# Reordering the projections around a hyena stage: memory products moved to the upper half's columns, backward states to the lower half's last columns, q taken last

## The chip, the cores and the metric

One core of a Trainium2 chip runs the whole layer. The engines are TensorE (PE, with its weight loads shown apart as PEld), VectorE (DVE), ScalarE (ACT), GpSimd (POOL) and SyncE (SP), whose queue issues most of the transfers; ScalarE's queue issues the others. The metric is the device time of one execution in microseconds; the time of a kernel is the median of its runs.

## The reference

A bidirectional encoder layer over 2048 tokens of width 1024, in float32. What matters here:

```python
u = _rms_norm(h, norm_mix_g[l])
proj = u @ w_in[l]                                    # hyena z, x1, x2 | q, k | v, o | gates
hy = _short_conv_centred(proj[..., :HY_COLS], ...)    # width 3, over tokens
y_hy = _group_rms_norm(_hyena(hy, spec, hy_skip[l]), hy_norm_g[l], HYENA_GROUPS)
qk = jax.nn.silu(_short_conv_centred(proj[..., HY_COLS:off], ...))
y_ml = _mlstm_bidirectional(q, k, v, o_pre, gates, ml_gate_b[l])   # chunkwise scan, both directions
h = h + concat(y_hy, y_ml) @ w_out[l]
h = h + _cross_attention(_rms_norm(h, norm_x_g[l]), _rms_norm(mem, norm_mem_g[l]), wq, wk, wv, wo)
h = h + jnp.square(jax.nn.relu(_rms_norm(h, norm_ff_g[l]) @ ff_w1[l])) @ ff_w2[l]
```

The hyena is two rounds of long convolution by Fourier transform, each multiplied by a gate (x1, then x2). The mLSTM is a linear recurrence over chunks of 128 tokens with a matrix state per head, once forward and once backward. The cross-attention reads 256 memory tokens; its key and value weights depend on the memory alone.

## The kernel before, in words

Every large product is split into a high and a low part in fp32r and done as three matmuls (`mm3`, L340 to L342). So each set of weights (`weights`, L359) is loaded in pieces of 256 KB, rounded to its high part on ScalarE and reduced to its low part on VectorE (`split`, L345). `stream` (L378) keeps one set ahead of the one in use, and the tags `wh` and `wl` have two buffers, so two sets exist at a time. The list `items` in `inproj_open` fixes the order in which sets are taken, and each consumer takes the next.

The work is written as Python generators, which yield a weight for what they have just emitted; `weave` (L1923) alternates between two of them by the ratio of the weights done, `among` (L1977) takes one step of a second generator after every few of the first. This gives the order of the program. A scheduler with a timing model then orders each engine's instructions: an instruction that comes later in the program can go first where the earlier one isn't ready. A few instructions are pinned to program order among themselves.

The input projection holds half of the tokens (1024) at a time as a split operand `xh`, `xl`. `sweep` (L657) computes groups of 256 columns with channels on partitions: for each group four blocks (two token halves by two column halves), each of 24 matmuls of 512 columns; then the short convolution (L704 to L711), and `sweep_out` (L714) for the store, put off by `pending` until a later block. Column groups 0 to 5 are the hyena inputs (4 and 5 are the gate x2), 6 and 7 are q, 8 and 9 are k. `natural` (L759) computes a group of 256 columns with tokens on partitions, eight row tiles of 24 matmuls with 256 columns: groups 0 and 1 are v, 2 and 3 are the output gate o, 3 with the gate columns. A natural group is called a natural tile below.

`memproj` (L602) works on the memory. For each of four heads and for keys, then values, a projection (`project`, 48 matmuls of 256 columns) is multiplied by a second set of weights (`keys`: 48 of 256 columns; `values`: 24 of 512) and stored as `gd` or `vw`, which attention reads as weights. The eight projections with their eight products take sixteen sets of weights of 1 MB.

`gates` prepares gate rows and columns for the mLSTM. `backward` (L1097) steps through the chunk states of the backward direction, from chunk 15 down, and stores each one: two transfers in, one product with the gate on GpSimd, eight matmul records (L1082), four VectorE updates (L1088), one transfer out. `mlstm` (L1115) then loads packed rows (L1142) and goes through chunks 0 to 15 with both directions at once: loads, scores (L1175), values and states (L1213, L1215), the forward state update, a norm.

Before, the order is: sweeps of groups 0 to 3 for both halves; then, woven with hyena by 279 to 499: groups 4 to 9 of the upper half, naturals 3, 0, 1, 2 of the upper half, natural 3 of the lower half, groups 4 to 9 of the lower half with a gate step after every third block, naturals 0 and 1 of the lower half, natural 2 and the first three projections with two key products, with the states of chunks 15 to 8 (`far_states`, L1111, pinned) among these. Behind hyena come the other memory products, woven with `mlstm`: first the states of chunks 7 to 1, whose old state is read back from memory (`old_state`), then chunks 0 to 4. The tiles of `mlstm` lie in the memory that hyena has used. Attention comes next, woven with the remaining chunks; it starts from the hyena half of its first 512 tokens and needs chunks 0 to 3 for the other half.

Of the kernel before, what the change touches and what calls it, by code (L numbers as in the profile page):

```python
# [10 lines left out]
F32 = mybir.dt.float32  # L11
# [9 lines left out]
D = 1024  # L21
# [112 lines left out]
class Prog:  # L134
# [249 lines left out]

    NAT_AT = {0: 2}

    def inproj_open(self, es):
# [195 lines left out]

    def prep_mem(self):
        sb = self.isb
        self.memt = [[sb.tile([128, 1088], F32R, tag=tag, name="mt", bufs=2)[:, 0:D].rearrange("p (k t) -> p k t", k=4)
                      for tag in ("P", "cv")] for h in range(2)]

        def load(h):
            t = sb.tile([128, D], F32, tag="xn", name="xt", bufs=2).rearrange("p (k t) -> p k t", k=4)  # L590
            self.nc.sync.dma_start(out=t, in_=self.a["mem_t"].rearrange("(k p) t -> p k t", p=128)[:, 4 * h:4 * h + 4])
            return t

        def halves():
            xs = [load(h) for h in range(2)]
            rb = self.spread(self.diagonal(self.rm))
            for h in range(2):
                self.scaled(xs[h], 4 * h, self.g_mem, rb, *self.memt[h])
                yield
        self.prepq = halves()  # L600

    def memproj(self):  # L602
        nc, sb = self.nc, self.isb
        gd = self.dram("gd", (2, 128, 8, 512))
        vw = self.dram("vw", (4, 128, 8, 256))
        self.pop(2)
        mt = self.memt

        def project():
# [6 lines left out]
            t = sb.tile([128, 2, 2, 256], F32R, tag="xn", name="kt", bufs=2)  # L616
            self.split(t[:, 0], t[:, 1], p)
            return t
# [471 lines left out]

    def old_state(self, sb, n):
        t = sb.tile([128, 4, 129], F32, tag="cf", name="cb", bufs=3)
        cbd = self.dram("cbd", (15, 128, 516))
        self.nc.sync.dma_start(out=t.rearrange("d h e -> d (h e)"), in_=cbd[n - 1])
        return t

    def backward(self, sb, first, last, old, pin=None, lean=False):  # L1097
# [12 lines left out]

    def far_states(self):  # L1111
        with self.tc.tile_pool(name="m_b", bufs=1, side="right") as sb:
            yield from self.backward(sb, 15, 7, None, self.tc.keep_in_program_order, True)

    def mlstm(self, es):  # L1115
# [23 lines left out]
        for s in range(2):  # L1139
# [801 lines left out]
def program(p):  # L1941
    with ExitStack() as ms:
        with ExitStack() as es:
            p.inproj_open(es)
            p.filters_open()
            p.prepq = p.x_first()
            p.pop()
            s = chain(p.sweep(range(4), 0, True, lambda: p.prep_x(1)), p.sweep(range(4), 1, False))
            next(s)
            next(s)  # L1950
            weave(s, p.filters(), 140, 80, True)
            p.gates_open(ms)
# [70 lines left out]
```

## Time and profile before

| What | Value |
|---|---|
| median of 3 runs | 3175.22 us (3166.64 to 3175.26) |
| the profiled execution | 3178.03 us |
| its span, first to last instruction | 3176.3 us |
| PE busy | 3039.3 us, 96% |
| PEld busy | 2393.8 us, 75% |
| DVE busy | 2048.0 us, 64% |
| ACT busy | 1503.0 us, 47% |
| POOL busy | 1157.8 us, 36% |
| mean granted clock of TensorE | 0.982 |
| moved by the DMA engines | 609.48 MB, 192 GB/s |

The page cuts the span into 40 slices of 79.4 us and gives for each the busy tenths of an engine, the granted clock and the DMA share. A second view gives busy times for any stretches; others list instructions in order of time, group them by line and shape, or tell for a tile what its instructions waited for. A wait is put down to the instruction that released it. Busy times of matmuls overlap, since their ends are modelled, so a price for TensorE is best taken from one start to the next.

### The profile page before, as it was taken

The page shows a single profiled execution, that of the slowest core. Times are in us where ns is not written, and L with a number is a line of the kernel's source. Part 1 is how long each engine was busy: PE and PEld are TensorE (multiplying, and loading weights), DVE is VectorE, ACT ScalarE, POOL GpSimd, SP SyncE. Part 2 cuts the span into 40 slices and gives each one's busy share as a digit, 9 for nine tenths or more (in the row PEclk, how much of TensorE's full clock was granted, in tenths as well). Part 3 has the DMA queues.
Part 4 walks back from the last instruction along what each step waited for, and adds up shares of the span by engine and source line. Part 5 has one row for each costly group of instructions (what it writes and reads, how often), then busy time and mean ns, then how long its engine had stood idle before and what let it go on. Part 6 is the DMA issues. An engine that isn't in the chain of part 4 may idle for free.

```text
span 3176.3 us, 43590 instructions
## 1 busy us (share of the span) xinstructions
PE 3039.3 (96%) x14473; PEld 2393.8 (75%) x14473; DVE 2048.0 (64%) x3563; ACT 1503.0 (47%) x2873; POOL 1157.8 (36%) x802
## 2 busy tenths in 40 slices
PE   6999999999999976999999999999999999999998
PEld 4655566776668766788888888888888878888876
DVE  7775466434865676878766566657655686565695
ACT  5543366523675343445454455556555443333335
POOL 0122012100112334324231426776555483434483
PEclk9999999999999998999999999999999999999999
DMA  5554767686576988547374747656644474444434
GB/s 190 191 196 162 255 194 205 180 253 212 165 226 191 309 256 263 172 144 231 114 272 144 274 131 246 203 194 221 216 155 146 163 243 147 144 129 152 123 93 169
DMA packets 447673, 609.48 MB, mean 192 GB/s; under 512 B 39118, under 2 KB 249166, under 8 KB 446424
## 3 DMA queue, kind: packets, MB, share of 16 engines
q1 hardware_dynamic: 409268, 548.18, 54.7%
q10 hardware_dynamic: 38180, 58.51, 5.5%
q8 instruction: 115, 1.88, 0.2%
q14 instruction: 110, 0.90, 0.1%
HBM read 404.15 MB, written 202.41 MB: 191 GB/s over the span
## 4 chain that ended last, share of the span: by engine, by line
PE 79%; DMA 8%; DVE 7%; issue 3%; ACT 2%; POOL 1%; SPq 0%; ACTq 0%; DVEq 0%; POOLq 0%
PE mm L340 17%; PE mm L342 17%; PE mm L341 17%; PE hy L342 5%; PE hy L340 5%; PE hy L341 5%; PE hy L177 3%; PE hy L876 2%; PE mm L845 2%; PE hy L918 1%; DMA xt<-in_x_t_dram 1%; DVE wl L345 1%; PE hy L1213 1%; PE hy L1082 1%; PE hy L1215 1%
## 5 line engine op out<-in xcount | busy, mean ns | idle before, releaser
L345 DVE TENSOR_TENSOR wl<-wn,wh 128x512 fp32r<-128x512 f32 (+1 forms) x364 | 289.5, 830 | 128.9 <-ACT wh L345 128.7
L1558 DVE TENSOR_TENSOR bl<-wr,bh 128x512 fp32r<-128x512 f32 x213 | 239.1, 1129 | 130.8 <-ACT bh L1557 130.6
L1557 ACT CAST ah<-w 128x512 fp32r<-128x512 f32 x284 | 176.7, 623 | 303.3 <-PE hy L341 156.1
L345 ACT CAST wh<-wn 128x512 fp32r<-128x512 f32 (+1 forms) x364 | 208.1, 619 | 218.7 <-PE mm L342 51.2
L923 POOL TENSOR_TENSOR b<-b,a 128x512 f32<-128x512 f32 x64 | 87.2, 1363 | 586.8 <-ACT b L921 463.2
L340 PE MATMUL mm<-xh,wh 128*128 128x512 f32 x640 | 271.6, 425 | 3.7 <-ACT xh L500 2.3
L341 PE MATMUL mm<-xl,wh 128*128 128x512 f32 x640 | 257.9, 404 | 2.4 <-DVE xl L345 1.8
L342 PE MATMUL mm<-xh,wl 128*128 128x512 f32 x640 | 259.2, 405 | 0.0
L1557 ACT CAST bh<-wr 128x512 fp32r<-128x512 f32 x232 | 143.7, 621 | 233.3 <-PE mm L342 181.1
L1558 DVE TENSOR_TENSOR al<-w,ah 128x512 fp32r<-128x512 f32 x236 | 214.4, 909 | 54.3 <-ACT ah L1557 52.9
L342 PE MATMUL mm<-bh,al 128*128 128x512 f32 x576 | 225.3, 394 | 7.3 <-DVE al L1558 4.7
L340 PE MATMUL mm<-bh,ah 128*128 128x512 f32 x576 | 226.9, 394 | 1.0 <-DVE acc L1715 0.9
L341 PE MATMUL mm<-bl,ah 128*128 128x512 f32 x576 | 226.1, 393 | 0.0
L340 PE MATMUL mm<-act,wh 128*128 128x512 f32 x512 | 198.4, 393 | 2.6 <-ACT wh L345 1.3
L341 PE MATMUL mm<-act,wh 128*128 128x512 f32 x512 | 200.4, 392 | 0.2 <-DVE act L345 0.2
L342 PE MATMUL mm<-act,wl 128*128 128x512 f32 x512 | 199.0, 391 | 0.0
L340 PE MATMUL hy<-bh,ah 128*128 128x512 f32 x448 | 175.2, 391 | 0.0
L341 PE MATMUL hy<-bl,ah 128*128 128x512 f32 x448 | 174.6, 390 | 0.0
L342 PE MATMUL hy<-bh,al 128*128 128x512 f32 x448 | 174.4, 390 | 0.0
L340 PEld LDWEIGHTS mm<-xh,wh 128*128 128x128 f32 x640 | 122.0, 191 | 65.7 <-issue 29.2
L341 PEld LDWEIGHTS mm<-xl,wh 128*128 128x128 f32 x640 | 121.6, 190 | 53.0 <-issue 24.4
L323 POOL TENSOR_TENSOR b<-b 128x512 f32<-128x512 f32 x32 | 59.1, 1848 | 275.8 <-DVE P L685 127.8
(378 smaller groups left out, 8487.2 us busy)
## 6 DMA issues: line engine op xcount, KB each, us to landing
wr<-hc SPq DMA_DIRECT2D x224, 256.0 KB
w<-in_ff_w_dram SPq DMA_DIRECT2D x172, 256.0 KB
hc<-wn SPq DMA_DIRECT2D x128, 256.0 KB
wn<-in_w_in_dram SPq DMA_DIRECT2D x100, 256.0 KB
hc<-q SPq DMA_DIRECT2D x96, 256.0 KB
fs<-a SPq DMA_DIRECT2D x32, 512.0 KB
a<-fs SPq DMA_DIRECT2D x64, 256.0 KB
a<-zs SPq DMA_DIRECT2D x64, 256.0 KB
```

The costliest lines, as they stand in the source:

```text
L177: b = self.nc.tensor.matmul(*products[-1], start=True, stop=True)
L323: nc.gpsimd.tensor_tensor(e[1], f, b, ALU.subtract)
L340: mm(ps, lh, rh, start=start, stop=False)
L341: mm(ps, lh, rl, start=False, stop=False)
L342: mm(ps, ll, rh, start=False, stop=stop)
L345: both = (self.nc.scalar.copy(hi, src), self.nc.vector.tensor_tensor(lo, src, hi.bitcast(F32), ALU.subtract))
L845: nc.tensor.matmul(pp, dm[:, m], t[:, m], start=True, stop=True)
L876: nc.tensor.matmul(pg, em[:, m], y, start=True, stop=True)
L918: nc.tensor.matmul(pp, dm[:, m], t[:, m], start=True, stop=True)
L923: nc.gpsimd.tensor_tensor(xt, xt, hi[:, m], ALU.mult)
L1557: self.nc.scalar.copy(hi, src)
L1558: eng.tensor_tensor(lo, src, hi.bitcast(F32), ALU.subtract)
```

## The change

- The memory's scaled operand (`mem_operand`, before `prep_mem`) gets tiles of its own in a pool beside hyena's, in place of the convolution's tags.
- All eight projections, the four key products and the value products of heads 0 and 1 are taken between the blocks of groups 4 to 9 of the upper half, one step after every third block (`both`). The projections of heads 2 and 3 for the values are stored (`vt`), and read back, split and multiplied behind hyena.
- The lower half's groups go 4, 5, 8, 9 (x2, k), with a gate step after every second block; then naturals 0 and 1 (v), with seven steps of backward states between; then groups 6 and 7 (q), with one step after each block. All fifteen states run there, pinned, without reading an old state back.
- Behind hyena stay natural 2 of the lower half and the two value products, beside chunks 0 to 4. The last store of q is flushed ahead of `mlstm`, which no longer steps through states.
- The ratios of `weave` follow: 279 to 565, and 38 to 48 behind hyena.

```diff
-        mem = first[:1]
-        for i in range(8):
-            mem += ([nat[self.NAT_AT[i]]] if i in self.NAT_AT else []) + first[i + 1:i + 2] + second[i:i + 1]
-        items = tr[:4] * 2 + tr[4:] + [nat[c] for c in (3, 0, 1, 2, 3)] + tr[4:] + nat[:2] + mem
+        (c4, c5, c6, c7, c8, c9), f, w = tr[4:], first, second
+        items = tr[:4] * 2 + [c4, c5, f[0], c6, f[1], w[0], f[2], w[1], c7, f[3], w[2], c8, f[4], w[3]]
+        items += [c9, f[5], w[4], f[6], w[5], f[7]] + [nat[c] for c in (3, 0, 1, 2, 3)]
+        items += [c4, c5, c8, c9] + nat[:2] + [c6, c7, nat[2]] + w[6:]
...
-    def prep_mem(self):
+    def mem_operand(self, pool):
         sb = self.isb
-        self.memt = [[sb.tile([128, 1088], F32R, tag=tag, name="mt", bufs=2)[:, 0:D].rearrange("p (k t) -> p k t", k=4)
-                      for tag in ("P", "cv")] for h in range(2)]
+        self.memt = [[pool.tile([128, 4, 256], F32R, name=f"mt{x}{h}") for x in "hl"] for h in range(2)]
...
+            if keep is not None:
+                nc.scalar.dma_start(out=vt[keep], in_=staged(p).rearrange("p i t -> p (i t)"))
+                return None
...
-        t = project()
-        for i in range(8):
-            if i in self.NAT_AT:
-                yield from self.natural(0, (self.NAT_AT[i],))
-            yield 11
-            nxt = project() if i < 7 else None
-            (keys if i < 4 else values)(i % 4, t)
-            t = nxt
+        with self.tc.tile_pool(name="m_t", bufs=1, side="right") as pool:
+            self.mem_operand(pool)
+            yield 0
+            t = project()
+            for i in range(6):
+                yield 11
+                nxt = project() if i < 5 else project(0)
+                (keys if i < 4 else values)(i % 4, t)
+                t = nxt
+            project(1)
+        yield 6
+        for i in range(2):
+            st = sb.tile([128, 512], F32, tag="st", name="st", bufs=3)
+            nc.sync.dma_start(out=st, in_=vt[i])
+            t = pair()
+            self.split(t[:, 0], t[:, 1], st.rearrange("p (i t) -> p i t", i=2))
+            values(2 + i, t)
+            yield 8
...
-    def far_states(self):
+    def back_states(self):
         with self.tc.tile_pool(name="m_b", bufs=1, side="right") as sb:
-            yield from self.backward(sb, 15, 7, None, self.tc.keep_in_program_order, True)
+            yield from self.backward(sb, 15, 0, None, self.tc.keep_in_program_order, True)
...
-        for _ in self.backward(sb, 7, 0, self.old_state(sb, 8)):
-            yield 3
...
-            n = p.memproj()
+            n, states = p.memproj(), p.back_states()
             with ExitStack() as hs:
                 weave(p.hyena(hs),
-                      chain(s, p.sweep(range(4, 10), 1, True), p.natural(1, (3, 0, 1, 2), lambda: p.prep_x(0)),
-                            p.natural(0, (3,)), among(p.sweep(range(4, 10), 0, False), p.gates(), 3),
-                            among(chain(p.natural(0, (0, 1), p.prep_mem, 2), take(n, 5)), p.far_states(), 1)),
-                      279, 499)
+                      chain(s, both(p.sweep(range(4, 10), 1, True), 3, take(n, 8)), p.natural(1, (3, 0, 1, 2), lambda: p.prep_x(0)),
+                            p.natural(0, (3,)), among(p.sweep((4, 5, 8, 9), 0, False), p.gates(), 2),
+                            both(p.natural(0, (0, 1)), 1, take(states, 7), 2), both(p.sweep((6, 7), 0, False), 1, states)),
+                      279, 565)
+            p.flush()
             m = p.mlstm(ms)
-            weave(n, take(m, 13), 85, 75)
-            for _ in take(m, 1):
-                pass
+            weave(chain(p.natural(0, (2,)), n), chain((12,), take(m, 6)), 38, 48)
...
+def both(g, n, h, m=1):
+
+    for i, v in enumerate(g):
+        yield v
+        if i % n == n - 1:
+            yield from take(h, m)
+    yield from h
```

More of the change, by code (lines that the diff above doesn't have):

```diff
@@ L383, in stream @@
         yield cur
-    NAT_AT = {0: 2}
     def inproj_open(self, es):
@@ L592, in load @@
             return t
[L594 to L600, printed above, removed]
+        xs = [load(h) for h in range(2)]
+        rb = self.spread(self.diagonal(self.rm))
+        for h in range(2):
+            self.scaled(xs[h], 4 * h, self.g_mem, rb, *self.memt[h])
     def memproj(self):
@@ L605, in memproj, with pair, project @@
         vw = self.dram("vw", (4, 128, 8, 256))
-        self.pop(2)
-        mt = self.memt
-        def project():
+        vt = self.dram("vt", (2, 128, 512))
+        def pair():
+            return sb.tile([128, 2, 2, 256], F32R, tag="xn", name="kt", bufs=2)
+        def project(keep=None):
+            mt = self.memt
             wh, wl = next(self.wst)
@@ L615, in project @@
                     self.mm3(p[:, m], wh[:, k, ms], wl[:, k, ms], mt[k // 4][0][:, k % 4], mt[k // 4][1][:, k % 4], k == 0, k == 7)
-            t = sb.tile([128, 2, 2, 256], F32R, tag="xn", name="kt", bufs=2)
+            if keep is not None:
+                nc.scalar.dma_start(out=vt[keep], in_=staged(p).rearrange("p i t -> p (i t)"))
+                return None
+            t = pair()
             self.split(t[:, 0], t[:, 1], p)
@@ L646, in values @@
                     nc.scalar.dma_start(out=vw[2 * d:2 * d + 2, :, 2 * h + mt].rearrange("i p c -> p i c"), in_=o)
-        t = project()
-        for i in range(8):
-            if i in self.NAT_AT:
-                yield from self.natural(0, (self.NAT_AT[i],))
-            yield 11
-            nxt = project() if i < 7 else None
-            (keys if i < 4 else values)(i % 4, t)
-            t = nxt
+        with self.tc.tile_pool(name="m_t", bufs=1, side="right") as pool:
[12 more added lines that the diff above has]
+            nc.sync.dma_start(out=st, in_=vt[i])
+            t = pair()
+            self.split(t[:, 0], t[:, 1], st.rearrange("p (i t) -> p i t", i=2))
+            values(2 + i, t)
+            yield 8
     def sweep(self, cols, hf, first, after=None):
@@ L1089, in update @@
                                                pc[:, 129 * i:129 * i + 129], ALU.mult, ALU.add)
[L1091 to L1095, printed above, removed]
     def backward(self, sb, first, last, old, pin=None, lean=False):
```

## The prediction

> **What bounds the kernel now.** I read the slices of the page first, then the busy table by stretches, then the instructions of TensorE and of SyncE's queue in order of time, and last the waits by tile. The slices show where TensorE is not full (slices of 79.4 us; busy tenths, then the granted clock):
>
> ```profile
> PE   6999999999999976999999999999999999999998
> ...
> PEclk9999999999999998999999999999999999999999
> ```
>
> Apart from the start there is one hole, in the fifteenth and sixteenth slice, 1112 to 1270 us. The same place by stretches, with one earlier stretch beside it for comparison (columns: length, then busy us and instructions of PE, weight loads, DVE, ACT, POOL; clock, DMA share, GB/s):
>
> ```profile
> core 0: us, PE busy (x) PEld busy (x) DVE busy (x) ACT busy (x) POOL busy (x), PEclk, DMA share, GB/s
> 1029.00:1157.00 128.00, 114.34 (x791) 96.24 (x790) 95.00 (x209) 45.14 (x85) 44.49 (x28) 0.96 0.93 283
> 1157.00:1230.00 73.00, 57.64 (x325) 50.31 (x323) 42.14 (x117) 32.03 (x80) 26.60 (x25) 0.88 0.93 292
> 1230.00:1285.00 55.00, 33.09 (x184) 30.46 (x184) 39.61 (x137) 19.47 (x82) 23.10 (x19) 0.69 0.62 199
> 340.00:510.00 170.00, 161.25 (x617) 105.73 (x610) 94.92 (x141) 96.09 (x154) 19.00 (x14) 0.98 0.75 232
> ```
>
> From 1029 to 1157 the memory products run beside the end of hyena, with the DMA engines at 0.93: TensorE is idle 13.7 us. From 1157 to 1285 it is idle 15.4 + 21.9 = 37.3 us, and its clock falls to 0.88 and 0.69. That second part is a chain, seen in the DMA queue of SyncE (start, us taken to issue):
>
> ```profile
> 1155.24 1.09 SPq L955 DMA_DIRECT2D yh<-a  x2
> ...
> 1160.06 7.44 SPq L1142 DMA_DIRECT2D rows<-rows  x8
> ...
> 1169.18 0.43 SPq L1064 DMA_DIRECT2D kn<-kn  x1
> ...
> 1203.91 0.33 SPq L1107 DMA_DIRECT2D cbd<-cb  x1
> 1204.28 0.43 SPq L1149 DMA_DIRECT2D qn<-qt  x1
> ```
>
> Hyena stores its last rows at 1155. Then come the packed rows (1160), then seven backward states one after the other (first load 1169, last store 1204), and only then the loads of chunk 0. TensorE's own order says what follows:
>
> ```profile
> 1223.44 0.39 PE L1213 MATMUL hy<-va,rw 128*128 128x129 f32 x2
> ...
> 1232.81 0.39 PE L1213 MATMUL hy<-va,rw 128*128 128x129 f32 x2
> ...
> 1254.15 0.64 PE L1213 MATMUL hy<-va,rw 128*128 128x129 f32 x2
> ...
> 1264.28 0.77 PE L1213 MATMUL hy<-va,rw 128*128 128x129 f32 x2 [1.23 <-issue]
> ...
> 1279.33 2.44 PE L1350 MATMUL hy<-ident,wn 128*128 128x128 f32 x16
> ...
> 1285.19 0.73 PE L340 MATMUL mm<-act,wh 128*128 128x512 f32 x2 [1.22 <-ACT act L345]
> ```
>
> Chunks 1 to 4 begin at 1223, 1233, 1254 and 1264, 9 to 21 us apart, and the first product of attention at 1285. So 1204 to 1285, 81 us, is five chunks by their own latency; the memory products that could cover it have run out by 1230.
>
> **The change, part by part.** Prices of TensorE work at full clock are spacings from start to start:
>
> ```profile
> 1002.05 0.28 PE L340 MATMUL mm<-wh,xh 128*128 128x256 f32 x1
> 1002.17 0.28 PE L341 MATMUL mm<-wl,xh 128*128 128x256 f32 x1
> ```
>
> and from the chain that ended last (start, us):
>
> ```profile
> 1151.21 0.21 PE mm L340
> ...
> 1005.59 0.89 PE hy L1082 x8
> ```
>
> 0.12 us for 256 columns, 0.215 for 512, 0.9 for one state. A projection or a key product is 48 x 0.12 = 5.8 us, a value product 24 x 0.215 = 5.2, a natural tile 192 x 0.12 = 23, a chunk about 5.3 (scores and state 0.9 each, 32 records at 0.11 between 1223.44 and the end of its group).
>
> 1. *What lies behind hyena's end.* Before, between 1157 and 1285:
>
> ```profile
> L1082 PE MATMUL hy<-ve,kn 128*128 128x129 f32 x96 | 17.1, 337 | 16.3 <-issue 9.7 <-POOL ve L1078 6.4 <-ACT hy L1218 0.2
> ...
> L342 PE MATMUL mm<-mt,wl 128*128 128x256 f32 x32 | 10.9, 342 | 0.6 <-DVE wl L345 0.2
> ...
> L340 PE MATMUL mm<-wh,kt 128*128 128x512 f32 x27 | 9.9, 449 | 0.8 <-ACT wh L345 0.8
> ```
>
> That is two projections (32 records of each of three kinds), most of four value products, seven states and five chunks: 11.6 + 20.8 + 6.3 + 26.5 = 65 us of work in 128. After, one natural tile, two value products and five chunks: 23 + 10.4 + 26.5 = 60. So only 5 us net moves ahead of hyena's end (+5); the gain cannot come from less work there but from a shorter chain.
>
> 2. *Seven states leave that chain.* They go beside the columns, so the 35 us from 1169 to 1204 fall away (-35). The 12 us from 1157 to 1169 (rows, masks) and the 81 us from loads to attention stay: 93 in place of 128. The reload of a stored state goes too; it is one DMA and inside the 35.
>
> 3. *q is now last, and chunk 0 reads it back.* The price of that trip (ns, min/median/max):
>
> ```profile
> L707 DVE SCALAR_TENSOR_TENSOR cv<-P,par,cv x9: 1286/1290/2359, 802.2 to 960.1; 128x1040 f32<-128x1040 f32 x9
> L704 ACT ACTIVATE cv<-P,par x8: 1252/1254/1261, 830.6 to 955.6; 128x1040 f32<-128x1040 f32 x8
> L709 ACT ACTIVATE cv<-cv x8: 1072/1074/1077, 838.0 to 961.4; 128x1040 f32<-128x1040 f32 x8
> ```
>
> and two transfers from the chain that ended last:
>
> ```profile
> 1188.12 5.01 DMA cbd<-cb
> ...
> 1206.04 6.14 DMA kk_t<-kt
> ```
>
> 1.25 + 2 x 1.29 + 1.07 + 5.0 + 6.1 = 16 us from the last q product to a loaded chunk. Chunk 0 would wait 12 + 6.1 = 18 for rows and its own load anyway, so I take 0. The natural tile (23 us) covers both on TensorE; without it the 16 would be idle. The flushed q store stands ahead of the loads in SyncE's queue: what queues behind it is only the chunk's loads, which need it.
>
> 4. *Six products, and two projections stored for later, go beside the columns.* Work is conserved, but the weight buffers are two: a column holds one for its four blocks, and a memory step pulled in between takes the next sets, so each of its 14 sets can be split only when the set before it is used up. Waits for weight sets in the memory stage of before (us, times), rows of the tile mt, then of kt:
>
> ```profile
>   DVE wl L345: 12.8, 20
>   ACT wh L345: 12.4, 13
> ```
>
> ```profile
>   ACT wh L345: 9.6, 9
> ...
>   DVE wl L345: 7.5, 7
> ```
>
> 42.3 us over 16 sets is 2.6 each, products and weight loads counted together and so an upper bound, at a DMA share of 0.93. In the new place the share was 0.75 and the column's other blocks are ready to run. Lower bound 0, upper 2.6; I take 0.7, nearer to 0, for the stretch 340:510 had only 8.8 us idle in 170 with the same kind of load (+10, ends 0 and +36). The transfers:
>
> ```profile
> wn<-in_xa_wk_dram SPq DMA_DIRECT2D x16, 256.0 KB
> ...
> gd<-o ACTq DMA_DIRECT2D x16, 256.0 KB
> ```
>
> 56 such pieces of weights, 16 of keys, 8 of values, the operand and the stored pairs are some 21.5 MB. At 232 GB/s over the 210 us of these columns 48.7 MB moved; with 21.5 more in 210 + 80 us of product time that is 242 GB/s, below the 283 of the saturated stretch. The two stored projections (0.5 MB out and back, one more split each) lie beside it and later beside the chunks: 0, or the two splits, 3 us, if that cover is gone.
>
> 5. *The end of hyena.* It now has a natural tile and the q columns beside it, one set of weights per 21 to 23 us of products where it had one per 5 to 6. Of the 13.7 us idle and 0.04 x 128 = 5 us of clock I take 10 back (-10, ends 0 and -19), for this end has hyena's own waits too.
>
> 6. *Seven more states are pinned in TensorE's order,* so a late one holds up what stands behind it there, hyena's pinned products too. All thirty updates of before:
>
> ```profile
>   issue: 22.1, 13
>   POOL ve L1078: 13.2, 4
> ```
>
> 1.2 us each, so 0 to 8 for seven; most of those waits fell in the starved stretch, so +3. The other moves (x2, k, v order, gates every second block, the operand in tiles of its own) keep their instructions and lie in stretches where TensorE is full: 0, up to 5 if gates are late.
>
> Sum: 5 - 35 + 0 + 10 - 10 + 3 = -27 us. The profiled execution took 3178.03, so 3151; it lies 2.8 above the median of 3175.22, so the forecast for the median is 3148.
>
> **The rivals.** *Same.* The chunks are covered no better than before: 33 us of products outside chunks and states against 32, and these now come early, while rows are loaded, so that nothing stands beside chunks 2 to 4. Four intervals from 1223 to 1279 took 56 us, 14 each. If each becomes the longest seen, 21, five take 105 in place of 70: the 35 are gone, and the time is 3148 + 35 = 3183. From half of that on, 17.5 us, it is within 9.5 of before. Against it: the 21 us interval came with the clock at half.
>
> *Slower: the held weight buffer.* Place: the 14 sets in the first columns. It decides from 27 + 9.5 = 36.5 us more than forecast, that is (10 + 36.5) / 14 = 3.3 us a set. For it: 2.6 was seen, and hyena's opening transfers fall on the first of these columns. At 4 us it is 56 in place of 10, 3148 + 46 = 3194. Against it: TensorE has column blocks and hyena products to do meanwhile, if the planned order puts them there. The Trainium skill (DMA: Bandwidth & Descriptors, "Issuing engines are not separate DMA queues") says that transfers issued by different engines share the same sixteen DMA engines, so the key and value stores on ScalarE's queue would compete with the loads; the share of 0.93 in the first stretch agrees.
>
> *Faster still.* If the natural tile and the values happen to fill the gaps, the clock stays up: the half-clock share of 1157 to 1285 was 0.12 x 2 x 73 + 0.31 x 2 x 55 = 52 us, worth up to 26; and chunks at 9 us intervals save some 20. Together with the rest near 3110. By the Trainium skill (TensorE: Matmul & The Clock Gate, Part 1) an idle window of some 3.4 us halves the clock and a busy one restores it; the clock of 0.69 where TensorE is idle 40% agrees. Against it: 60 us of work cannot fill 93.
>
> **How the numbers follow.** Forecast 0.58, with its own range 3125 to 3165; same 0.12; slower 0.23; faster still 0.07. A change under 0.3% (9.5 us) cannot be told from none. Faster 0.58 + 0.07 = 0.65, same 0.12, slower 0.23. The range goes from 3118, leaving half of the fastest case, to 3194, the slower rival at its price, leaving the worse half of it.
>
> **What would show it.** Step 2: first loads of q some 12 us behind hyena's last store, and attention's first product some 93 us behind it. Step 4: products of the memory tile between 350 and 650 us, with waits for wl and wh of some 10 us. Step 5: TensorE full up to hyena's last store, some 8 us later than at 1155. It is wrong if the columns beside the products stretch by more than 45 us beyond their work, if the fifteen states end after q, or if five chunks take over 100 us.

## The result, and the profile after

The change made the kernel slower. The median after is 3208.49 us (5 runs, 3206.24 to 3213.8) against 3173.32 before in the same comparison (3166.64 to 3175.26), a ratio of 1.012 with a 95% interval of 1.0102 to 1.0138. The forecast was 3148 us, faster, in a range from 3118 to 3194. The two profiled spans are 3204.5 and 3176.3 us; the profiled execution after is the fastest of its five (3206.24), the one before took 3178.03.

The first view is that of the slices, of the kernel after (busy tenths, then the granted clock):

```profile
PE   6999899989999984899999999999999999999998
...
PEclk9999999999999997999999999999999999999999
```

The hole has not gone. It is deeper: the sixteenth slice, 1202 to 1282 us, is 0.4 busy, with 0.8 on either side, and the ninth, from 641 us, now shows 0.8. The same by stretches, the kernel after (length, then busy us and instructions of PE, weight loads, DVE, ACT, POOL; clock, DMA share, GB/s):

```profile
core 0: us, PE busy (x) PEld busy (x) DVE busy (x) ACT busy (x) POOL busy (x), PEclk, DMA share, GB/s
340.00:575.00 235.00, 220.97 (x1028) 156.88 (x1028) 136.23 (x203) 140.07 (x238) 28.80 (x22) 0.97 0.81 246
575.00:700.00 125.00, 103.44 (x466) 76.80 (x465) 63.04 (x97) 62.06 (x106) 13.08 (x10) 0.95 0.75 216
700.00:1103.00 403.00, 389.98 (x2172) 296.66 (x2171) 224.18 (x446) 193.08 (x341) 50.86 (x39) 1.00 0.69 201
1103.00:1207.00 104.00, 91.83 (x498) 71.70 (x497) 60.01 (x155) 32.64 (x52) 35.53 (x24) 0.94 0.88 265
1207.00:1237.00 30.00, 10.50 (x45) 5.84 (x43) 16.00 (x49) 2.97 (x6) 11.26 (x8) 0.73 0.64 196
1237.00:1334.00 97.00, 62.92 (x374) 57.63 (x375) 78.80 (x239) 41.55 (x156) 48.96 (x41) 0.78 0.66 206
```

and the kernel before from the same start, same columns (its fourth stretch, to 1157, stands in the prediction):

```profile
340.00:575.00 235.00, 222.03 (x890) 148.36 (x883) 136.03 (x205) 136.74 (x222) 32.88 (x24) 0.99 0.74 225
575.00:700.00 125.00, 122.34 (x828) 100.52 (x827) 52.47 (x84) 49.87 (x95) 10.48 (x8) 1.00 0.73 212
700.00:1029.00 329.00, 316.92 (x1471) 227.42 (x1470) 204.88 (x399) 183.09 (x303) 48.49 (x36) 0.98 0.68 199
```

SyncE's queue, in order of time, gives the landmarks of the kernel after (start, us taken to issue):

```profile
1143.14 1.12 SPq L965 DMA_DIRECT2D yh<-a  x2
...
1211.47 0.33 SPq L1111 DMA_DIRECT2D cbd<-cb  x1
1213.06 1.09 SPq L965 DMA_DIRECT2D yh<-a  x2
1228.00 6.84 SPq L965 DMA_DIRECT2D yh<-a  x4
1237.51 5.31 SPq L1146 DMA_DIRECT2D rows<-rows  x8
1242.86 0.45 SPq L1151 DMA_DIRECT2D qn<-qt  x1
```

The row at 1228.00 merges the stores of the seventh and the eighth closing step. The same view from 1231 us on begins with the last pair:

```profile
1233.75 1.09 SPq L965 DMA_DIRECT2D yh<-a  x2
```

The view of the tile `act` gives the first product of attention, here for the kernel after (ns min/median/max, first and last start):

```profile
L340 PE MATMUL mm<-act,wh x512: 387/389/501, 1313.5 to 1936.6; 128*128 128x512 f32 x171
```

A fourth landmark is the last product of hyena's second transform, since the eight closing steps that lead to its stores (transform back, gate, group norm, store) can only begin behind it. The view of the tile `em`, for the kernel after and then the kernel before:

```profile
L886 PE MATMUL hy<-b,em x128: 590/592/1224, 416.6 to 1105.4; 128*128 128x512 f32 x128
```

```profile
L876 PE MATMUL hy<-b,em x128: 590/592/697, 417.6 to 1023.2; 128*128 128x512 f32 x128
```

Call these E (that product), S (the stores of the last hyena rows), Q (first load of a chunk) and F (attention's first product). From F to the end of the span both kernels take 1891 us (3204.5 - 1313.5 and 3176.3 - 1285.2), so F tells the whole difference between the profiled executions, 28.3 us; the medians differ by 35.

The account against the start at 340 us: the packed rows came at 1160 and come at 1237.5. Taken to just ahead of them, 1157 and 1237, the four stretches of before hold 775.6 us of TensorE work and 41.4 idle, the five of after 816.7 and 80.3. That is 41 more of work and 39 more of idle time: 19 of it in 575 to 700 (21.6 against 2.7), 18 at the end of hyena (12.2 + 19.5 from 1103 to 1237, against 13.7). From there to F it is 76.5 us in place of 128.2, 52 less. So 41 + 39 - 52 = 28 us. Up to E alone, which comes 82 us later, the same view gives 716.8 us of work in 765.4 us after and 655.5 in 683.2 before: 61 of the 82 are work, 21 are idle time.

### The profile page after: what moved, and what is told of

Its sections match the earlier page's. It is cut to its first block, busy times and chain, and to the rows that moved or that the text cites. A ratio compares the mean times of both kernels' runs of the same rounds, so it can differ in the third digit from the quotient of the medians.

```text
span 3204.5 us, 43565 instructions
## 1 busy us (share of the span) xinstructions
PE 3034.6 (95%) x14473; PEld 2390.5 (75%) x14473; DVE 2040.3 (64%) x3563; ACT 1500.7 (47%) x2874; POOL 1148.7 (36%) x802
## 4 chain that ended last, share of the span: by engine, by line
PE 52%; DVE 4%; DMA 2%; issue 2%; ACT 1%; POOL 1%; SPq 0%; DVEq 0%; POOLq 0%; ACTq 0%
PE mm L340 11%; PE mm L342 11%; PE mm L341 11%; PE hy L340 5%; PE hy L342 5%; PE hy L341 5%; DVE bl L1560 1%; PE hy L1215 1%; PE hy L1217 1%; DVE acc L1881 0%; PE hy L1177 0%; PE hy L1092 0%; DVE acc L1847 0%; PE hy L1463 0%; DMA wr<-hc 0%
## 5 line engine op out<-in xcount | busy, mean ns | idle before, releaser
L345 DVE TENSOR_TENSOR wl<-wn,wh 128x512 fp32r<-128x512 f32 (+1 forms) x364 | 279.0, 805 | 148.2 <-ACT wh L345 147.8
L933 POOL TENSOR_TENSOR b<-b,a 128x512 f32<-128x512 f32 x64 | 84.4, 1319 | 658.5 <-ACT b L931 481.3
L340 PE MATMUL mm<-wh,xh 128*128 128x256 f32 (+1 forms) x512 | 151.5, 296 | 7.8 <-ACT wh L345 4.6
```

The lines of the kernel that those rows point to most:

```text
L340: mm(ps, lh, rh, start=start, stop=False)
L345: both = (self.nc.scalar.copy(hi, src), self.nc.vector.tensor_tensor(lo, src, hi.bitcast(F32), ALU.subtract))
L933: nc.gpsimd.tensor_tensor(xt, xt, hi[:, m], ALU.mult)
```

## The experiments

Landmarks and medians of all runs. Medians of before in their batches were 3170.14 to 3174.15, and the ratios are to these. The landmarks are of the one profiled execution of each kernel.

| kernel | E | S | Q | F | E to F | median | ratio [95%] |
|---|---|---|---|---|---|---|---|
| before | 1023 | 1155 | 1204 | 1285 | 262 | 3173.32 | 1 |
| after | 1105 | 1234 | 1243 | 1313.5 | 208 | 3208.49 | 1.012 [1.0102, 1.0138] |
| states alone | 1021 | 1186 | 1200 | 1283 | 262 | 3175.77 | 1.0014 [1.0004, 1.0024] |
| products alone | 1107 | 1214 | 1255 | 1327 | 220 | 3223.59 | 1.0164 [1.0149, 1.018] |
| edges | 1080 | 1213 | 1222 | 1292 | 212 | 3185.43 | 1.0044 [1.0029, 1.0059] |
| ratio 320 | 1044 | 1190 | 1222 | 1296 | 252 | 3189.63 | 1.0063 [1.0046, 1.008] |
| edges, ratio 320 | 1056 | 1203 | 1235 | 1309 | 253 | 3197.93 | 1.0087 [1.007, 1.0103] |
| the same, no pin | 1053 | 1203 | 1234 | 1309 | 256 | 3199.34 | 1.0094 [1.0078, 1.011] |
| after, no pin | 1108 | 1236 | 1246 | 1317 | 208 | 3210.16 | 1.013 [1.0114, 1.0146] |
| states alone, no pin | 1017 | 1182 | 1194 | 1277 | 260 | 3176.01 | 1.0022 [1.001, 1.0033] |
| after, hyena's end first | 1105 | 1239 | 1248 | 1319 | 213 | 3215.43 | 1.0129 [1.0113, 1.0146] |
| before, hyena's end first | 1019 | 1154 | 1204 | 1280 | 261 | 3176.45 | 1.0008 [0.9997, 1.0019] |
| after, no group norm | 1108 | 1192 | 1205 | 1287 | 179 | 3179.51 | 1.0022 [1.0011, 1.0032] |
| before, no group norm | 1023 | 1131 | 1181 | 1272 | 249 | 3166.64 | 0.9983 [0.9973, 0.9994] |
| after, short products | 1068 | 1199 | 1208 | 1281 | 212 | 3173.63 | 1.0003 [0.9991, 1.0015] |
| before, short products | 1018 | 1149 | 1194 | 1274 | 256 | 3167.60 | 0.9981 [0.9971, 0.9992] |
| states spread | 1024 | 1167 | 1179 | 1274 | 249 | 3161.85 | 0.9958 [0.9944, 0.9973] |

**The two halves of the change, each alone.** First, the kernel before with all fifteen states ahead of the end of hyena, and nothing else:

```diff
-            yield from self.backward(sb, 15, 7, None, self.tc.keep_in_program_order, True)
+            yield from self.backward(sb, 15, 0, None, self.tc.keep_in_program_order, True)
...
-        for _ in self.backward(sb, 7, 0, self.old_state(sb, 8)):
-            yield 3
...
-            weave(n, take(m, 13), 85, 75)
+            weave(n, take(m, 5), 85, 75)
```

> One part alone, on the kernel before: all fifteen backward states run pinned beside the end of hyena and the memory products, nothing else is moved. Theory A (the time is set by a chain: end of hyena's products, its norm steps, then rows, states, chunks; a step taken out of that chain is won): the 35 us of the seven states fall out behind hyena's last store, which itself comes some 6 us later for the 6 us of work put ahead of it, so about 3173 - 29 = 3144. Theory B (the loss is in the first columns, in the waits for weight sets, and the chain matters little): within 5 of 3144 as well, so this run does not part A from B; it parts both from theory C (pinned states hold TensorE up wherever they are put), by which the 35 come back as waits ahead of the pinned products: 3170 or more.

Second, the kernel after with the states of chunks 7 to 1 put back behind hyena, as they were:

```diff
-            yield from self.backward(sb, 15, 0, None, self.tc.keep_in_program_order, True)
+            yield from self.backward(sb, 15, 7, None, self.tc.keep_in_program_order, True)
...
+        for _ in self.backward(sb, 7, 0, self.old_state(sb, 8)):
+            yield 3
...
-            weave(chain(p.natural(0, (2,)), n), chain((12,), take(m, 6)), 38, 48)
+            weave(chain(p.natural(0, (2,)), n), chain((12,), take(m, 14)), 38, 75)
```

> The changed kernel with the states of chunks 7 to 1 put back behind hyena, as before, so that the products and the column order are moved alone. Theory A: hyena's end stays at about 1237 us less some 6, and the states come back into the chain with nothing to cover them, so 3208 + 29 = 3237. Theory B: the moved products are what costs and the states are nothing, 3208 or a little less.

The states alone gained nothing: 3175.77, as theory C had it. The products alone, with the new order of the columns, lost more than the whole change: 3223.59, half way between the two theories. SyncE's queue in the kernel with the states alone shows where their gain went:

```profile
1115.46 1.11 SPq L955 DMA_DIRECT2D yh<-a  x2
...
1126.85 1.13 SPq L955 DMA_DIRECT2D yh<-a  x2
1132.12 0.63 SPq L1107 DMA_DIRECT2D cbd<-cb  x1
...
1151.18 0.34 SPq L1107 DMA_DIRECT2D cbd<-cb  x1
1176.41 1.13 SPq L955 DMA_DIRECT2D yh<-a  x2
1185.99 1.20 SPq L955 DMA_DIRECT2D yh<-a  x2
...
1200.27 0.39 SPq L1147 DMA_DIRECT2D qn<-qt  x1
```

Hyena's rows come every 11 to 22 us up to 1127; then states are stored, one behind the other, and the seventh store of hyena follows 50 us behind the sixth. From S to F it is 97 us in place of 130, as predicted; but S is 31 us later. In the pair with the products, where E is the same to 2 us, the states shorten S to F from 113 to 80 and put S 20 us later. So the states do leave the chain, for 33 us in both pairs, and most of that comes back ahead of S.

**The pin.** The prediction had the pinned order as the way in which states hold hyena up. The same two kernels with the states not pinned, that is:

```diff
-            yield from self.backward(sb, 15, 0, None, self.tc.keep_in_program_order, True)
+            yield from self.backward(sb, 15, 0, None, None, True)
```

> The kernel before with all states moved ahead, as in the first experiment, and not pinned. That one had hyena's seventh and eighth store at 1176 and 1186 with seven states stored between 1120 and 1151, where the kernel before had them at 1145 and 1155. Theory P: they come back to about 1155, the chain behind them stays short, and the time is 3145 to 3150. Theory Q: no change from 3176.

> The changed kernel with the fifteen states not pinned; all else as it is. Theory P (hyena's last pinned products stand in TensorE's order behind pinned states, and each state waits for the one before it): hyena's last store comes 15 to 30 us earlier than 1228 and the time falls to about 3185. Theory Q (the last steps are late by their place in the program and on VectorE and GpSimd, the pin does not matter): 3200 to 3210.

The pin is not it: 3176.01 and 3210.16 us, against 3175.77 and 3208.49 with it, as theory Q had it.

**The states, spread.** If it is not the pin, it may be that the steps stand in a heap. The kernel before again with all fifteen states ahead, two steps behind each block; they still count at no weight in the ratio with hyena:

```diff
-                            among(chain(p.natural(0, (0, 1), p.prep_mem, 2), take(n, 5)), p.far_states(), 1)),
+                            both(p.natural(0, (0, 1), p.prep_mem, 2), 1, take(far, 7), 2), both(take(n, 5), 1, far, 2)),
...
-            n = p.memproj()
+            n, far = p.memproj(), silent(p.far_states())
...
+def silent(g):
+    for _ in g:
+        yield 0
```

> The kernel before with all states moved ahead, now two steps after each block, so that none of them stands in a heap ahead of hyena's seventh and eighth step, which came 40 us late in both kernels with states alone. Theory D with the heap as cause of that delay: S at about 1160 in place of 1187, attention some 95 behind it, 3145 to 3155. If S stays near 1185 the states take their place wherever they stand, and the time stays at 3172 to 3176.

This one is faster than both kernels: 3161.85 us, ratio 0.9958 [0.9944, 0.9973]. SyncE's queue in it:

```profile
1141.06 1.10 SPq L955 DMA_DIRECT2D yh<-a  x2
1155.26 1.11 SPq L955 DMA_DIRECT2D yh<-a  x2
1167.36 1.09 SPq L955 DMA_DIRECT2D yh<-a  x2
1172.34 6.82 SPq L1142 DMA_DIRECT2D rows<-rows  x8
1179.20 0.48 SPq L1147 DMA_DIRECT2D qn<-qt  x1
```

The gap of 50 us is gone. S is 12 us later than before in place of 31, and F 11 us earlier, which falls short of what was expected (S at 1160, 3145 to 3155 us). The states also end earlier, the last one stored at 1133 in place of 1151, and which of the two counts was not tested. That is what the idea of moving the states is worth here: a third of the 35 us, since hyena's end still pays for them and S to F is 106 us, not 97.

**Where the products are taken.** Each column group holds one set of weights for four blocks; in the kernel after the memory steps fall inside the groups. Here they come only between two groups, with the list of weights in that order:

```diff
-        items = tr[:4] * 2 + [c4, c5, f[0], c6, f[1], w[0], f[2], w[1], c7, f[3], w[2], c8, f[4], w[3]]
+        items = tr[:4] * 2 + [c4, f[0], c5, f[1], w[0], c6, f[2], w[1], c7, f[3], w[2], c8, f[4], w[3]]
...
-                      chain(s, both(p.sweep(range(4, 10), 1, True), 3, take(n, 8)),
+                      chain(s, *(g for c, k in zip(range(4, 10), (2, 1, 1, 1, 1, 2)) for g in (p.sweep((c,), 1, True), take(n, k))),
```

> The changed kernel with the memory steps taken only between two column groups, when no group holds a weight buffer, in place of after every third block. Theory B (the held buffer costs the 17 us of TensorE's waits for wh and wl between 560 and 700): those waits go and the time is about 3190; if the buffer is the whole of the loss, 3173 or less. Theory A: the waits may go, but hyena's last step comes when its own chain and its place in the order let it: 3200 to 3208.

A second kernel changes only the ratio of the weave, so that hyena runs ahead:

```diff
-                      279, 565)
+                      320, 565)
```

> The changed kernel with hyena woven in at 320 to 565 in place of 279 to 565, so that hyena is emitted earlier and some 65 of the 565 units of other work stand behind its end. Theory A (hyena's last eight steps come too late and run out bare, 1207 to 1237, with the cover used up before): the last store comes some 40 us earlier and the hole closes, about 3180. Theory B: nothing in the first columns changes, 3205 or more.

The edges took the time to 3185.43, 23 us less. The two stretches from 340 to 700, in the kernel with the edges (columns as above):

```profile
340.00:575.00 235.00, 226.02 (x1065) 162.03 (x1064) 145.79 (x221) 144.96 (x242) 28.40 (x22) 0.99 0.82 246
575.00:700.00 125.00, 113.39 (x588) 90.40 (x587) 60.39 (x106) 64.77 (x114) 13.16 (x10) 0.93 0.76 229
```

TensorE is idle 11.6 us in the second in place of 21.6, and 9.0 in place of 14.0 in 340 to 575: 15 of the 23 us are waits that have gone, as theory B had it, but the time is not down to 3173, so they are not the whole loss. The list of waits of the kernel after in 575 to 700 names what they were (in total, times, longest):

```profile
PE mm L340 <- ACT wh L345: 14.1, 6, 4.6
...
ACT wh L345 <- DMA wn<-in_xa_wv_dram: 9.2, 3, 3.5
ACT wh L345 <- DMA wn<-in_w_in_dram: 8.5, 3, 5.4
```

TensorE waited for sets of weights to be split. In the two longest of these waits the split had itself just waited for its weights to land, though the DMA share was 0.75 (rows of TensorE and of ScalarE, the wait in brackets):

```profile
678.26 0.62 ACT L345 CAST wh<-wn 128x512 fp32r<-128x512 f32 x1 [3.34 <-DMA wn<-in_xa_wv_dram]
...
678.93 0.39 PE L340 MATMUL mm<-mth,wh 128*128 128x256 f32 x1 [4.63 <-ACT wh L345]
...
694.17 0.64 ACT L345 CAST wh<-wn 128x544 fp32r<-128x544 f32 x1 [5.43 <-DMA wn<-in_w_in_dram]
...
694.87 0.82 PE L340 MATMUL mm<-wh,xh 128*128 128x272 f32 x2 [4.64 <-ACT wh L345]
```

Whether those transfers were late because a held buffer let them start late is not shown.

The ratio alone took off 19 us: E came at 1044 in place of 1105, and E to F grew from 208 to 252. SyncE's queue in that kernel shows why E to F grew:

```profile
1190.50 1.14 SPq L965 DMA_DIRECT2D yh<-a  x2
...
1205.34 9.18 SPq L1111 DMA_DIRECT2D cbd<-cb  x3
...
1216.77 5.29 SPq L1146 DMA_DIRECT2D rows<-rows  x8
```

Here the states end behind hyena, the last one stored at 1214, and the packed rows come only after it, 26 us behind S. A ratio of 380 to 565 was meant to show how far this goes, and gave no time. The two edits together did worse than either:

> Both edits that helped at once: memory steps only between column groups, and hyena woven in at 320 to 565. If they mend different losses (the held buffer, -23; hyena's late end, -19) they add to about 3167; if both act on the same hole at hyena's end, about 3183.

> The same with unpinned states. Theory P: a further 10 to 20 below that run, 3150 to 3160, below both kernels. Theory Q: as that run.

3197.93 and 3199.34 us. Two steps worth 23 and 19 us alone gave 11 together, with E at 1056, not earlier than with the ratio alone, and here too the packed rows (1230) wait for the last state (1227), 27 us behind S. Why E is later than with the ratio alone I have not found, so single moves of 10 us in this table should not be read as prices.

**The end of hyena, put first.** In the kernel after, 31.7 us of TensorE are idle between 1103 and 1237, and S comes 128 us behind E; before it was 132. One theory was that hyena's closing steps lose against the other work on VectorE and GpSimd. Here the whole body of these steps gets precedence in the scheduler:

```diff
-                js = slice(2 * j2, 2 * j2 + 2)
-                r, gate = nxt
+                with tc.high_priority(3000) if o else nullcontext():
+                    js = slice(2 * j2, 2 * j2 + 2)
+                    r, gate = nxt
...
```

> The changed kernel with hyena's last eight steps (gate, norm, store) given precedence over other work in the planned order. Landmarks so far: from the last transform product E to hyena's last store S 132 us before and 128 after; from S to the first attention product F 130 and 80. Theory L (E to S is the eight steps' own latency, whatever stands beside them): S and the time stay, 3205. Theory O (other work stands ahead of the steps): S comes 30 us earlier or more, the natural tile and the value products are left over as cover for the chunks, and the time falls to 3180 or below.

> The same precedence in the kernel before. Theory L: no change from 3170. Theory O: S comes some 30 us earlier there too, but the seven states and the memory products still stand behind it, so 3150 to 3160.

Nothing came of it: S is at 1239 in place of 1234, and at 1154 in place of 1155. Then the closing steps without the group norm, the rows being stored as they are gated:

```diff
-                y = gate.rearrange("q j (g e) -> q (j g) e", g=8)
...
-                nc.gpsimd.tensor_tensor(sqv, y, y, ALU.mult)
...
-                nc.vector.tensor_reduce(ms, sqv, AX.X, ALU.add)
-                rv = self.bank_rsqrt(sb, ms, 64)
-                nc.vector.tensor_tensor(sqv, y, rv.unsqueeze(2).broadcast_to([128, 16, 64]), ALU.mult)
-                for jj in range(2):
-                    nc.gpsimd.tensor_tensor(sq[:, jj], sq[:, jj], ghy, ALU.mult)
...
-                    nc.sync.dma_start(out=yh[g, :, js], in_=sq[own[g]])
+                    nc.sync.dma_start(out=yh[g, :, js], in_=gate[own[g]])
```

> The changed kernel without the group norm of hyena's result (square, sum, root, two multiplications of each of the last eight steps are left out, the gated rows are stored as they are). Theory L (the eight steps' own chain makes E to S): E to S falls to some 60 us and the time by 40 or more, to 3165. Theory O: E to S is set by what else runs, 110 or more, and the time falls by less than 15.

> The same left out in the kernel before. Theory L: S comes some 60 us earlier but the memory products fill the time from E on, so the time falls less than in the changed kernel, 15 to 25, to about 3150. Theory O: less than 10.

S came 42 us earlier in the kernel after and 24 in before; the time fell by 29, between the two theories, and by 5.5, on the side of theory O. From E to S it is now 84 us in the kernel after, of which TensorE is busy 80.8, so there it can't be much shorter. So what sets E to S is in good part the chain of the norm on GpSimd and VectorE. In the kernel after some two thirds of it are on the path, since little is left to run beside it; before, TensorE's memory products ran under it and most of its length was free.

**The same work, in its two places.** The pair that bears most on the loss. Both kernels with the memory products cut short: the projections take one of eight steps of their sum, the keys and values one of two.

```diff
-                for k in range(8):
-                    self.mm3(p[:, m], wh[:, k, ms], wl[:, k, ms], mt[k // 4][0][:, k % 4], mt[k // 4][1][:, k % 4], k == 0, k == 7)
+                self.mm3(p[:, m], wh[:, 0, ms], wl[:, 0, ms], mt[0][0][:, 0], mt[0][1][:, 0], True, True)
...
-                    for m in range(2):
-                        self.mm3(p[:, i], qh[:, m, ds], ql[:, m, ds], t[:, 0, m], t[:, 1, m], m == 0, m == 1)
+                    self.mm3(p[:, i], qh[:, 0, ds], ql[:, 0, ds], t[:, 0, 0], t[:, 1, 0], True, True)
...
-                    for m in range(2):
-                        self.mm3(p, t[:, 0, m, ms], t[:, 1, m, ms], oh[:, m, ds], ol[:, m, ds], m == 0, m == 1)
+                    self.mm3(p, t[:, 0, 0, ms], t[:, 1, 0, ms], oh[:, 0, ds], ol[:, 0, ds], True, True)
```

> What a microsecond of product is worth at the place it was moved to. The changed kernel with the memory products cut short: one of eight terms of each projection and one of two of each key and value product is computed, all weights, splits and stores stay, the rest of the terms is left out. That takes 41 + 11.6 + 5.2 = 58 us of TensorE's work out of the first columns and 5 from the end. Theory D (what is put ahead of hyena's last transform E delays E and all behind it by its full length, while from E to attention the eight steps, rows and chunks set the pace): E comes some 58 earlier and the time falls by 50 to 60, to 3150 to 3158. Theory B (the waits for weight sets, not the products, stretch the first columns): falls by less than 40.

> The same terms left out of the kernel before, where 63 us of the same work lie between E and attention. Theory D: they are cover for the eight steps, the states and the chunks, so the time falls by 30 or less, to 3143 or more. If work counts the same at both places, it falls by 55 to 65.

By the prices of the prediction this takes out 8 x 42 x 0.12 + 4 x 24 x 0.12 + 4 x 12 x 0.215 = 62 us of TensorE work, of which 57 lie ahead of E in the kernel after (all but two value products). Before, all of it lies behind E: the view of the tile `mt` there has its first product at 1029.2, E being 1023.2:

```profile
L340 PE MATMUL mm<-mt,wh x128: 277/283/416, 1029.2 to 1201.0; 128*128 128x256 f32 x128
```

Without it the kernel after falls from 3208.49 to 3173.63, 35 us; the kernel before only from 3174.15 to 3167.60, 6.5 us. A microsecond of these products costs some 0.6 ahead of E, and 0.1 behind it; the 0.1 is hardly told from nothing, for in the shortened kernel before E itself came 5 us earlier, with none of these products ahead of it. The shortened pair differ by 6 us in place of 35, so the place of these products makes up 29 of the 35. The edges alone took back 23 of the same 35, so the two overlap and can't be added. The 35 us are less than the 50 to 60 of theory D. From 340 us to E the shortened kernel after has 53 us less of work, but 16 more of idle time (664.0 busy of 728.5); the weights had stayed as they were:

```profile
340.00:575.00 235.00, 202.07 (x773) 132.89 (x771) 149.01 (x217) 150.53 (x254) 32.00 (x23) 0.94 0.85 256
575.00:700.00 125.00, 106.01 (x526) 78.88 (x527) 58.98 (x101) 59.45 (x106) 12.47 (x9) 0.92 0.78 231
```

In 340 to 575 it is idle 32.9 us in place of 14.0, in 575 to 700 still 19.0. So the work taken out counts in full up to E, and idle time takes 16 us of it back. In the shortened kernel before TensorE is idle 39.7 of the 130.7 us from E to S, at a granted clock of 0.75, and E to S is as long as with the whole products (132): there they were cover.

## Why the prediction was wrong, by its own steps

**The bound.** The prediction took the hole between 1157 and 1285 as what there is to shorten, and hyena's last store at 1155 as a point that the change moves by 8 us. What it left out is why that store stands at 1155. It stands 132 us behind E, and in after still 128, though less TensorE work lies between (99.9 us in place of 118.3), in good part because the eight closing steps have a chain of their own. Behind it come the chunks with theirs. Of the kernels with the complete norm none has less than 208 us from E to F, and cutting the products short did not bring it below that (212); whether another order could was not tried. Before there were 262. The change brought E to F down to 208; but it put its products ahead of E, and E came 82 us later: 82 - 54 = 28. In the terms of the sum, measured up to the packed rows and behind them: step 1 was 41 us in place of 5, step 4 was 20 in place of 10, steps 5 and 6 were 18 in place of -7, step 2 was -52 in place of -35, and 1 us lies elsewhere: 28 in place of -27.

**Step 1, work behind hyena's end (+5): failed, and it is the largest term.** I counted a natural tile and two value products, 33 us, as work behind hyena. Nothing holds them there: they need weights, the value products also their stored projection, and a free TensorE, and the scheduler ran them beside the closing steps. The natural tile's and the value products' rows in the kernel after, by the tiles `xh` and `kt`:

```profile
L340 PE MATMUL mm<-wh,xh x512: 278/283/691, 684.4 to 1178.2; 128*128 128x256 f32 x128, 128*128 128x272 f32 x43
```

```profile
L340 PE MATMUL mm<-wh,kt x32: 387/408/796, 604.6 to 1213.6; 128*128 128x512 f32 x32
```

The last ones start at 1178 and 1214, ahead of S (1234). So 41 us more of work lies ahead of the packed rows (5 + 33, and 3 that I can't place), not 5. The 33 us are then missing beside the chunks, which did not take longer for it. Holding the tile back behind hyena wasn't tried on the chip.

**Step 2, seven states leave the chain (-35): right, and more.** The chain that ended last, in the kernel after, around that point (start, us):

```profile
1234.25 3.19 DMA yh<-a
1237.51 0.74 SPq L1146
...
1245.74 5.71 DMA kk_t<-kt
1251.58 2.05 PE hy L1177 x8
```

The last rows are in memory at 1237.4; the first load of a chunk is issued 5 us later (forecast 12), and attention begins 76 us later (forecast 93, before 128). S to F shrinks by 33 us with the states in both pairs of kernels with and without them, which is the size of the step; the rest of the 52 came with the other moves. The rival that the five chunks would stretch, *Same*, did not happen: from the first load to attention it is 1313.5 - 1242.9 = 71 us, where it was 81 before and would have been 116 by that rival.

**Step 3, q last (0): right.** The first load of q is issued at 1242.86, the moment SyncE has issued the packed rows (1237.51 + 5.31). The view of the tile `qt` has the last store of q 79 us ahead of it, so nothing waits for that trip:

```profile
L746 SPq DMA_DIRECT2D qt<-cv x8: 325/330/557, 463.2 to 1164.1; - x8
```

**Step 4, products beside the columns (+10): right mechanism, size off by two.** TensorE's idle time in 340 to 700 grew by 1.1 + 18.9 = 20 us, 1.4 a set in place of 0.7, and taking the steps to the edges of the groups brought back 23. That is the mechanism of the rival *Slower*, but at 1.4 to 1.6 a set and not at the 3.3 from which it would have decided. The waits are a part of the loss and not the whole: the kernel with the edges is still 0.44% slower than before. The half of step 4 that failed outright is a sentence: "Work is conserved". It is, but work ahead of E is paid at 0.6 and the same work behind E at 0.1.

**Step 5, the end of hyena (-10): wrong sign.** I took the 13.7 us idle there as lack of TensorE work. They became 31.7. From E to S, in the kernel with the products alone and in the kernel after (columns as above):

```profile
1107.10:1213.60 106.50, 90.16 (x477) 67.28 (x475) 71.04 (x170) 35.07 (x57) 37.96 (x25) 0.96 0.80 250
1105.40:1233.80 128.40, 99.92 (x533) 76.03 (x531) 76.02 (x204) 35.01 (x57) 46.79 (x32) 0.90 0.85 256
```

Without the seven states 16.3 us are idle there, with them 28.5: 12 us of the idle time came with step 6. The runs without the norm show that the closing steps' own chain is another part; precedence did not shorten it.

**Step 6, seven more states (+3): too small, and for the wrong reason.** S is 20 us later with them than without (the products alone against the whole change); in the kernel before it is 31 later when they stand in a heap and 12 when spread. The pin has no part in it that shows. That they compete for VectorE and GpSimd with hyena's closing steps fits the 50 us gap and the spread kernel; it was not measured by itself.

The sum, from 340 us on: forecast +5 +10 -10 +3 = +8 for S, measured +80 to the packed rows; forecast -35 behind it, measured -52. Of the three signs given for a wrong prediction one came true: the fifteen states end after q. The last store of q is issued at 1164, and five states are stored after it, the last at 1211, beside hyena's last steps. The other two did not: the columns beside the products waited 20 us more, not 45, and the chunks took 71 us, not 100. The prediction had watched for waits, and 61 of the 82 us by which E moved are work. The rise of the clock hoped for in *Faster still* did not come; in the worst stretch the rows of the kernel after show 0.73 and 0.78.

## What to carry to other kernels

Before taking work from one place to another, ask which point starts the latency chain that ends the stage, and whether the work lies ahead of or behind that point: behind it, such work was nearly free here (0.1), ahead of it, it cost more than half of its length (0.6). Where a scheduler orders the instructions, work that waits for nothing need not stay where the program puts it, so it can't be counted as cover for something later. Steps that are moved beside a chain on other engines should be spread through it, or end ahead of it, and not stand in a heap; here that made the difference between no gain and 0.42%.

## What the runs showed that was not expected

- From E to S it takes 128 to 135 us in the kernels before, after, with edges and with precedence, though before has the memory products there and the others have only two value products of them. But it is no constant: with the products moved and the seven states not, it is 107, with the states in a heap 165, and leaving out the norm brings it to 84 (after) and 108 (before).
- Precedence and pins, which change the order on paper, moved the medians by 7 us at most, and the intervals with and without them overlap.
- Two separate improvements of the kernel after, 23 and 19 us alone, gave 11 us together. With the ratio the states end behind hyena and hold up the packed rows; why E comes 12 us later with both edits than with the ratio alone is open.
